# Moving the context norm behind the first latent products, pipelining the shifts in place, and spilling the values in 2 KB rows, in a hybrid attention layer

## The chip, the cores and the metric

The kernel runs on one core of one Trainium2 chip. The metric is the device time of one execution in microseconds (us). An execution is one launch of the whole layer: the inputs lie in the chip's memory, and the output is written back to it.

## The reference

One backbone layer over 512 latent tokens and 256 context tokens, all of width 2048, in f32. Two mixers read the same modulated norm: differential attention (8 heads of 128, two softmax maps per head) and multi-head latent attention (8 heads, low-rank q and kv). Behind them stand one output projection and a gated MLP with a depthwise convolution. Cut to what the change touches (the names are the reference's):

```python
mod_x = (silu(c) @ w_ada + b_ada)          # 6 x 2048: shift, scale, gate, twice
mod_c = (silu(c_ctx) @ w_ada + b_ada)      # the same for the context
h  = rmsnorm(x,   norm1_w) * (1 + s1)  + sh1     # latents,  512 x 2048
hc = rmsnorm(ctx, norm1_w) * (1 + s1c) + sh1c    # context,  256 x 2048
p  = h @ w_in ; pc = hc @ w_in                   # 3776 columns, one combined projection
q_da, k_da, v_da, c_q, c_kv, k_rope = split(p)   # the context's likewise
k_all = concat(context keys, latent keys) ; v_all = concat(context values, latent values)
w = softmax(q1 @ k1.T * a) - lam * softmax(q2 @ k2.T * a)     # per head
o_da = w @ v_all
x = x + g1 * (concat(rmsnorm(o_da) * .., o_mla) @ w_o)
h2 = rmsnorm(x, norm2_w) * (1 + s2) + sh2
x = x + g2 * ((silu(conv3(h2 @ w_up[:, :5632])) * (h2 @ w_up[:, 5632:])) @ w_down)
return rmsnorm(x, final_w)
```

## The kernel before

**Arithmetic.** Activations lie transposed, features on the 128 partitions, in 16 K-tiles (`kt`) of 128 features. A product of f32 accuracy is made of three: each operand is split into a high part (an ACT copy that rounds, lines 80, 210, 236, 386) and a low part (a DVE subtraction, lines 81, 213, 242, 389), and `mm3` issues high·high, high·low and low·high (lines 107, 108, 109). So nearly every weight block costs one 512 KB load by SP, one ACT cast, one DVE subtraction, and some tens of products on PE.

**Order.** The first stages stand inside `tc.manual_schedule`, which keeps on each engine the order in which the program issues the instructions. An engine works its list strictly in order, so what is written first runs first, and a late instruction holds up all behind it. Later stages, the attention and the output projection among them, are ordered by the scheduler of the language.

**Start.** SP loads the latents (16 tiles `xs`, 256 KB each), then the first rows of the scale weights (`scale_load`, 8 x 256 KB, tiles `adak`), two weight blocks and the 8 context tiles `cs`. ACT squares each tile (`sum_square`, lines 334 and 340), DVE adds the squares up in one tile (342), PE multiplies what is left with ones to sum over partitions (349), and `root` makes the reciprocal root `rinv`. The modulation's scale for a pair of K-tiles `u` is worked out by `scale_products(u)` on PE (285), a copy to `row` on ACT (290), `scale_turn` on PE (296) and `scale_out` on DVE (302).

**Projection of the first five column blocks (g0).** `g0_mm(kt, which)` (line 391) multiplies K-tile `kt` of the weights with the latents (`which` has 0) or the context (1), into PSUM tiles `lat0`, `ctx0`. It goes round by round, `u` = 0 to 7, two K-tiles a round. In each, DVE scales the next pair (`scaled`, 381), splits it (242; 244 where a shift is added) and makes the low parts of the weights (389).

**Row sums.** The shift of the modulation is a matrix-vector product on DVE: `row_sums` (line 260) multiplies a 1 MB row block of `w_ada` with the wide silu vectors `cb` (latents) and `ccb` (context) and sums along the row, 2.35 us each, 32 in all, one per K-tile and vector. The row blocks (tiles `ada`, two buffers, in POOL's queue) can't be loaded before the Silu of `ccb` is done, since a POOL copy into `gate` stands ahead of them in the queue. The K-tiles 8 to 15 get their shift with their split; 0 to 7 get it later, in place, by `add_shift` (line 594), before their products of the value columns. For the five g0 blocks, and the first half of block 5, which were multiplied without it, `bias_products` (line 643) multiplies the shift with those weights once more and adds it as a bias.

**Steps.** From there the projection goes in steps. `step(block, *tasks)` issues the products of weight block i, the cast of block i+2, the first task, the low part of block i+2, the load of block i+4, and then the other tasks. Steps 0 and 1 are `half_feature` (8.4 us each), steps 2 to 9 the eight `value_block`s, 10 and 11 `block(1,0)` and `block(1,1)`, 12 `block(2,0)`, then `bias_products(0)`, step 13 `block(2,1)`, and so on. The values of the first four heads, in six PSUM areas `v0` (two `b` tiles and the four halves of two `s` tiles), are split and written to the scratch array `v_d` by `put_value` (line 602) beside steps 10 and 11. A `gemv` (line 169) is the same as a row sum for the other modulation rows: 1 MB loaded, 2.4 us of DVE (174). 38 of them stand in the projection, each a task of a step (`gemvs(1)`). A small DVE instruction at line 1064 makes the scale of the second norm out of each.

**Later.** Attention reads v_d head by head (`da_head`, loads at line 872). The output projection (from line 1030 on) has weight blocks `w_o` of 5.44 us of PE each, with a gemv (`next_gemv(wo, 1)`, line 1046) before most of them; SP loads both.

## Time and profile before

| what | us |
|---|---|
| median of 3 runs (2431.09 to 2436.43) | 2435.21 |
| profiled execution | 2432.03 |
| its span, first to last instruction | 2430.2 |
| PE busy | 2332.7 (96%) |
| DVE busy | 1779.8 (73%) |
| ACT busy | 1102.3 (45%) |
| POOL busy | 273.2 (11%) |

The span and what lies around it (1.8 us) make the profiled execution. PE is busy in 96% of the span, and the granted TensorE clock is 0.989 on average. Rows of a timeline give start, duration (us), engine, line, operation, output and inputs, the shape, and in brackets how long the engine had stood idle before and which engine's instruction released it.

### The profile page before, as it was taken

To read this page: it belongs to the slowest core of one execution; us is meant where nothing else is said; L and a number is where in the kernel's file an instruction comes from. 1 tells how busy PE (TensorE), PEld (TensorE's weight loads), DVE (VectorE), ACT (ScalarE), POOL (GpSimd) and SP (SyncE) were. 2 spreads that over 40 slices of the span, in tenths; PEclk is the share of its full clock that TensorE was granted. 3 is DMA by queue.
4 is the path that set the end of the run, shared out by engine and by line. 5 is a ranking of instruction groups with operands and counts; after the bars stand their busy time and mean duration, and the time that the engine had idled before them with its cause. 6 is when DMAs were issued, how large, how long until landed. Compare 5 with 4: busy or idle time off the path is not lost.

```text
span 2430.2 us, 32271 instructions
## 1 busy us (share of the span) xinstructions
PE 2332.7 (96%) x12408; PEld 1962.5 (81%) x12408; DVE 1779.8 (73%) x2305; ACT 1102.3 (45%) x1660; POOL 273.2 (11%) x324
## 2 busy tenths in 40 slices
PE   5989799999999999989999999999999999999997
PEld 3777588777677778888888888888888888888887
DVE  5997577698868777587676767676766667676667
ACT  5222132255555542254454444454545445454553
POOL 0000100121200002100101011111111111111113
PEclk9999899999999999999999999999999999999999
DMA  9865877854411159723546555555555555555572
GB/s 356 298 234 192 299 253 285 281 158 119 134 51 44 44 212 372 260 83 114 152 118 156 121 156 122 156 122 156 122 154 124 147 131 141 137 137 141 133 214 79
DMA packets 139338, 407.45 MB, mean 168 GB/s; under 512 B 14752, under 2 KB 31664, under 8 KB 128560
## 3 DMA queue, kind: packets, MB, share of 16 engines
q1 hardware_dynamic: 105120, 298.42, 37.1%
q0 software_dynamic: 32912, 105.93, 18.2%
q8 instruction: 97, 1.59, 0.3%
q10 hardware_dynamic: 1152, 1.05, 0.1%
q14 instruction: 57, 0.47, 0.1%
HBM read 335.86 MB, written 69.48 MB: 167 GB/s over the span
## 4 chain that ended last, share of the span: by engine, by line
PE 78%; DVE 8%; issue 7%; DMA 3%; ACT 3%; POOL 1%; SPq 0%; DVEq 0%; POOLq 0%; ACTq 0%
PE y L1314 12%; PE b L108 9%; PE b L107 9%; PE b L109 9%; PE z L1314 6%; PE y L1316 6%; PE z L1316 3%; PE s L830 3%; PE x L1314 2%; PE s L108 2%; PE s L109 2%; PE s L107 2%; PE f L107 1%; PE x L1316 1%; PE pt L842 1%
## 5 line engine op out<-in xcount | busy, mean ns | idle before, releaser
L1335 POOL DMA_DIRECT2D x_d<-xs x160 | 140.4, 1014 | 1163.0 <-ACT xs L1334 1144.1
L107 PE MATMUL b<-ah,wh 128*128 128x512 f32 (+1 forms) x672 | 259.1, 386 | 0.0
L108 PE MATMUL b<-al,wh 128*128 128x512 f32 (+1 forms) x672 | 259.0, 385 | 0.0
L109 PE MATMUL b<-ah,wl 128*128 128x512 f32 (+1 forms) x672 | 258.0, 384 | 0.0
L1290 DVE TENSOR_TENSOR wl<-wr,wh 128x1024 fp32r<-128x1024 f32 x126 | 153.7, 1220 | 129.0 <-ACT wh L1284 129.0
L1290 DVE TENSOR_TENSOR wl<-rb,wh 128x1024 fp32r<-128x1024 f32 x124 | 151.1, 1219 | 127.9 <-ACT wh L1284 127.9
L1284 ACT CAST wh<-wr 128x1024 fp32r<-128x1024 f32 x126 | 132.3, 1050 | 206.1 <-PE b L108 100.4
L1284 ACT CAST wh<-rb 128x1024 fp32r<-128x1024 f32 x124 | 130.2, 1051 | 187.9 <-PE b L108 112.3
L1290 DVE TENSOR_TENSOR wl<-ws,wh 128x1024 fp32r<-128x1024 f32 x123 | 150.0, 1220 | 88.9 <-ACT wh L1284 88.9
L174 DVE CUSTOM_DVE_ANT_0 ada<-ada,cb,smt 128x2048 f32<-128x2048 f32 x64 | 153.7, 2405 | 55.0 <-DMA ada<-in_ada 54.1
L1284 ACT CAST wh<-ws 128x1024 fp32r<-128x1024 f32 x123 | 128.2, 1042 | 136.0 <-PE b L108 45.3
L109 PEld LDWEIGHTS b<-ah,wl 128*128 128x128 f32 x672 | 126.3, 188 | 25.6
L107 PEld LDWEIGHTS b<-ah,wh 128*128 128x128 f32 x672 | 126.6, 188 | 23.0
L108 PEld LDWEIGHTS b<-al,wh 128*128 128x128 f32 x672 | 126.6, 188 | 21.9
L107 PE MATMUL b<-a2k,wh 128*128 128x512 f32 (+1 forms) x352 | 136.5, 390 | 7.1 <-ACT a2k L1097 5.1
L109 PE MATMUL b<-a2k,wl 128*128 128x512 f32 (+1 forms) x352 | 134.3, 382 | 7.2 <-DVE wl L213 7.2
L80 ACT CAST wh<-wr 128x1024 fp32r<-128x1024 f32 (+2 forms) x64 | 64.3, 1005 | 135.0 <-PE b L108 42.9
L832 DVE TENSOR_REDUCE m<-s 128x1 f32<-128x768 f32 x96 | 90.2, 949 | 22.9 <-PE s L830 22.6
L1314 PE MATMUL y<-b2k,wh 128*128 128x512 f32 x410 | 106.9, 390 | 0.0
L210 ACT CAST wh<-wr 128x1024 fp32r<-128x1024 f32 x38 | 39.9, 1049 | 141.5 <-PE s L108 46.1
L1334 ACT ACTIVATE xs<-b,modx 128x512 f32<-128x512 f32 x160 | 101.1, 681 | 2.3 <-DMA x_d<-xs 1.9
L81 DVE TENSOR_TENSOR wl<-wr,wh 128x1024 fp32r<-128x1024 f32 (+2 forms) x64 | 78.3, 1223 | 32.3 <-ACT wh L80 31.9
(534 smaller groups left out, 6082.7 us busy)
## 6 DMA issues: line engine op xcount, KB each, us to landing
rb<-in_w_up SPq DMA_DIRECT2D x123, 512.0 KB, 4.5
ada<-in_ada POOLq DMA_DIRECT2D x54, 1024.0 KB, 5.6
wr<-in_w_dn SPq DMA_DIRECT2D x84, 512.0 KB, 4.0
x_d<-xs POOLq DMA_DIRECT2D x160, 256.0 KB, 6.0
wr<-in_w_up SPq DMA_DIRECT2D x53, 512.0 KB, 4.3
ada<-in_ada SPq DMA_DIRECT2D x26, 1024.0 KB, 6.7
wr<-in_w_f SPq DMA_DIRECT2D x34, 512.0 KB, 5.7
adak<-in_ada_k SPq DMA_DIRECT2D x64, 256.0 KB, 5.3
```

The source lines that it names most:

```text
L81: ve.tensor_tensor(dst_l, src, dst_h.bitcast(F32), op=ALU.subtract)
L107: pe.matmul(out, st[0], mv[0], start=start, stop=False, **kw)
L108: pe.matmul(out, st[0], mv[1], start=False, stop=False, **kw)
L109: pe.matmul(out, st[1], mv[0], start=False, stop=stop, **kw)
L174: ve.tensor_tensor_reduce(out=junk, in0=w, in1=vec, op0=ALU.mult, op1=ALU.add, scale=1.0, scalar=col("b_ada", j), accum_out=dst[:, j:j + 1])
L832: ve.tensor_reduce(out=m, in_=s[:, :TT], axis=AX.X, op=ALU.max, negate=True)
L1284: sc.copy(hi, raw)
L1290: ve.tensor_tensor(lo, raw, hi.bitcast(F32), op=ALU.subtract)
L1314: pe.matmul(o, w[j][0], hs[j], start=start and j == 0, stop=False, skip_group_check=True)
L1316: pe.matmul(o[:, h0], w[j][1], hs[j][:, h0], start=False, stop=j == 7, skip_group_check=True)
L1334: sc.mul(x, po, modx[:, 80 + dt:81 + dt])
L1335: gp.dma_start(x1_d[dt], x, accum_op=ALU.add)
```

## The change

Seven things are moved or reshaped; the arithmetic stays.

1. **Norm of the latents.** The last four squares go to PE directly, one ones-product each (345), so that DVE adds 11 tiles and not 14. The second half of the context loads comes behind `scale_load(1)`. `scale_products(0)` stands ahead of `root(0)`. `keep_warm` issues products of no use (cpad times ones, 7 x 512 columns, then 2 x 256 and 8 x 256) into a PSUM tile that is overwritten later.
2. **Norm of the context.** It moves behind the latent products of K-tiles 0, 1 and 2, and round 0 is folded into what comes before the loop. DVE adds all eight squares; `ctx_sum` needs two ones-products, where there were four. The Silu of `cb` and `ccb` comes behind the casts of K-tiles 2 and 3.
3. **Row sums.** Rounds 5 and 6 take two in place of three. In round 7 the low parts of the first two step blocks come ahead of their sums. More sums stand in step 0 and in the first value blocks.
4. **Shifts.** `add_shift` adds into a tile `sh` of its own, and issues the sums of the next pair before the low parts of the one before it; its K-tiles are spread over value blocks 1 to 5 as [0], [1], [2, 3, 4], [5, 6], [7], with row sums or gemvs in between.
5. **Values.** `v_d` is laid out as [high or low, key tile, 128, 512], so that one write has rows of 512 numbers, 2 KB, where a write had pieces of 128. A head's read becomes two reads with pieces of 128. Two of the six splits use tiles of their own (`rt`), in place of a pair that an earlier write must leave first.
6. **Bias weights.** Their loads are issued a step ahead (`bias_load`).
7. **Gemvs.** 36 stand in the projection, where 38 did; two move to the output projection, whose condition becomes `if kb != 7 if g else kb`.

```diff
@@ -338,28 +341,38 @@ the norms
-            if j < (15, 7)[i]:
-                ve.tensor_tensor(s, s, sq, op=ALU.add)
+            if i == 0 and j > 11:
+                pe.matmul(g0b[1], ones32, sq, start=j == 12, stop=False)
+                if j == KT - 1:
+                    pe.matmul(g0b[1], ones32, s, start=False, stop=True)
                 return
...
+            ve.tensor_tensor(s, s, sq, op=ALU.add)
+        def keep_warm(count, cols):
+            for _ in range(count):
+                pe.matmul(lat0[0][:, :cols], ones32, cpad.rearrange("p k i -> p (k i)")[:, :cols], start=True, stop=True)
...
+        keep_warm(7, 512)
         for kt in range(KT):
             sum_square(0, kt, xs[kt])
         sc.preload_act_table_set(tables)
+        scale_products(0)
+        scale_load(1)
+        ctx_load(range(4, 8))
+        keep_warm(2, 256)
         root(0)
-        scale_products(0)
         row = scale_row(0)
         scale_turn(0, row)
         scale_out(0)
+        keep_warm(8, 256)
@@ -406,27 +419,60 @@ ahead of the rounds
+        g0_mm(0, (0,))
+        scale_products(1)
...
+        g0_mm(1, (0,), (4, 0))
+        scale_turn(1, row)
+        g0_mm(1, (0,), (1, 2, 3))
...
+        ctx_sum()
         root(1)
+        g0_mm(2, (0,))
+        scale_products(2)
...
         g0_mm(0, (1,))
         g0_mm(1, (1,))
...
+        for wide in (cb, ccb):
+            sc.activation(wide, wide, AF.Silu)
+        sc.preload_act_table_set(tables)
         gp.tensor_copy(gate, ccb[:, 0:1])
         for kt in row_order[:2]:
             row_load(kt)
@@ -444,40 +490,32 @@ the rounds
-            elif u < NU - 1:
-                row_sums(3)
+            if u < NU - 1:
+                row_sums(3 if u < 5 else 2)
             else:
                 for i in range(2):
                     load(i)
                 for i in range(2):
                     cast(i)
-                    row_sums(2)
                     low(i)
                     load(i + 2)
-                row_sums(1)
+                    row_sums(2)
@@ -591,19 +629,27 @@ shifts and values
+    def add_shift(kts, between=None):
+        late = []
         for kt in kts:
...
+            t = kvs.tile([P, TT], F32, tag="kh", name=nm("sh"))
+            for hl, m, c in ((hx[kt], modx, slice(0, T)), (hc[kt], modc, slice(T, TT))):
+                ve.tensor_tensor(t[:, c], hl[0].bitcast(F32), hl[1].bitcast(F32), op=ALU.add)
+                high(hl, t[:, c], m[:, kt:kt + 1])
+                late.append((hl, t[:, c], m[:, kt:kt + 1]))
+            if len(late) > 2:
+                for _ in range(2):
+                    rest(*late.pop(0))
...
-            nc.sync.dma_start(v_d[half][:, :, i, t].rearrange("h p d -> p h d"), g.bitcast(F32))
+            nc.sync.dma_start(v_d[half][i, t], g.bitcast(F32))
@@ -725,16 +776,19 @@ steps 10 to 17
-        a, b, c, d, e_, f_ = lay(first)
-        step(block(1, 0), a, b, gemvs(1), c)
-        step(block(1, 1), d, gemvs(1), e_, f_, gemvs(1))
-        step(block(2, 0), feature_keys(1, gemvs(1)))
+        step(block(1, 0), lay(0), lay(5), gemvs(1), lay(1, True))
+        step(block(1, 1), lay(2), lay(3), gemvs(1), lay(4, True))
+        bias_load(0)
+        step(block(2, 0), gemvs(1), feature_keys(1))
         bias_products(0)
@@ -869,7 +923,9 @@ a head's values
-        nc.sync.dma_start(v.bitcast(F32), v_d[h // 4][h % 4])
+        for i in range(2):
+            nc.sync.dma_start(v[:, i].bitcast(F32),
+                              v_d[h // 4][i][:, :, h % 4 * P:(h % 4 + 1) * P].rearrange("t p d -> p t d"))
@@ -1042,7 +1098,7 @@ the output projection
-            if kb != 7 if g else kb > 2:
+            if kb != 7 if g else kb:
                 next_gemv(wo, 1)
```

How this moves the instructions shows at three places. The first is DVE's list at the end of the g0 rounds. `junk` and `ada` rows at line 260 are the row sums, the row at 389 (402 in the change) is the last low part of a g0 block, and the row at 213 the low part of step 0's weights. Before:

```order
L389 TENSOR_TENSOR wl_1301<-wr_1217,wh_1300 128x640
L260 ISA junk_1304,modx<-ada_1209,cb,smt 128x2048
L260 ISA modx 128x1
L260 ISA ada_1209,modc<-ada_1209,ccb,smt 128x2048
L260 ISA modc 128x1
L260 ISA junk_1309,modx<-ada_1294,cb,smt 128x2048
L260 ISA modx 128x1
L260 ISA ada_1294,modc<-ada_1294,ccb,smt 128x2048
L260 ISA modc 128x1
L260 ISA junk_1375,modx<-ada_1307,cb,smt 128x2048
L260 ISA modx 128x1
L213 TENSOR_TENSOR wl_1370<-wr_1365,wh_1369 128x1024
```

and in the change:

```order
L402 TENSOR_TENSOR wl_1317<-wr_1231,wh_1316 128x640
L260 ISA junk_1320,modx<-ada_1225,cb,smt 128x2048
L260 ISA modx 128x1
L260 ISA ada_1225,modc<-ada_1225,ccb,smt 128x2048
L260 ISA modc 128x1
L213 TENSOR_TENSOR wl_1384<-wr_1379,wh_1383 128x1024
```

Five sums stood between the two subtractions, and two stand there now; over all rounds 21 sums come before step 0's low part, and now 18.

The second place is DVE's list beside steps 10 to 12, where the values are split: rows at line 81 are the low parts of the values, from the PSUM tiles `s` and `b`, rows at 174 are gemvs, the one at 213 is a step's low part. Before:

```order
L81 TENSOR_TENSOR kl_2051<-s_1544,kh_2050 128x512
L1064 SCALAR_TENSOR_TENSOR a_93<-modx,smt 128x1 x2
L81 TENSOR_TENSOR kl_2108<-s_1544,kh_2107 128x512
L213 TENSOR_TENSOR wl_2105<-wr_1974,wh_2104 128x1024
L174 ISA ada_2116,modx<-ada_2116,cb,smt 128x2048
L174 ISA modx 128x1
L81 TENSOR_TENSOR kl_2120<-s_1545,kh_2119 128x512
```

and in the change:

```order
L81 TENSOR_TENSOR rt_2053<-s_1558,rt_2052 128x512
L1120 SCALAR_TENSOR_TENSOR a_93<-modx,smt 128x1
L81 TENSOR_TENSOR kl_2110<-s_1558,kh_2109 128x512
L213 TENSOR_TENSOR wl_2107<-wr_1976,wh_2106 128x1024
L81 TENSOR_TENSOR kl_2119<-s_1559,kh_2118 128x512
L174 ISA ada_2124,modx<-ada_2124,cb,smt 128x2048
L174 ISA modx 128x1
```

The third split goes to tiles `rt` of its own and no longer needs the `kl` of the first; the split of the second `s` tile's first half now stands ahead of a gemv.

The third place is SP's list at the change to the second half of the output projection: `ada` rows are 1 MB gemv rows, `wr` rows the weight blocks. Before:

```order
L171 DMA ada_7890<-in_ada 128x2048
L171 DMA ada_7957<-in_ada 128x2048
L89 DMA wr_7960<-in_w_o 128x1024
L171 DMA ada_7990<-in_ada 128x2048
L89 DMA wr_7993<-in_w_o 128x1024
L1055 DMA xr_7945<-in_x_t 128x512
```

and in the change:

```order
L171 DMA ada_7840<-in_ada 128x2048
L171 DMA ada_7873<-in_ada 128x2048
L89 DMA wr_7976<-in_w_o 128x1024
L171 DMA ada_7906<-in_ada 128x2048
L171 DMA ada_7973<-in_ada 128x2048
L1111 DMA xr_7961<-in_x_t 128x512
L89 DMA wr_8009<-in_w_o 128x1024
L171 DMA ada_8006<-in_ada 128x2048
L171 DMA ada_8039<-in_ada 128x2048
L89 DMA wr_8042<-in_w_o 128x1024
```

Two rows of 1 MB stand between neighbouring weight blocks at two places, where one stood.

More of the change, by code (lines that the diff above doesn't have):

```diff
@@ L147, in layer_kernel @@
     k_d = [dram.tile([2, P, TT], F32, name=f"k_d{h}") for h in range(NH)]
-    v_d = [dram.tile([4, P, 2, NKEY, P], F32, name=f"v_d{i}") for i in range(2)]
+    v_d = [dram.tile([2, NKEY, P, 512], F32, name=f"v_d{i}") for i in range(2)]
     def apply_rope(out, ps, tmp):
@@ L306, in layer_kernel, with ctx_load @@
         raws_ = [wraw(w_g0[kt], 640) for kt in range(2)]
-        for i in range(8):
-            cs.append(c2k())
-            nc.sync.dma_start(cs[i], ctx_t[i])
-        scale_load(1)
+        def ctx_load(n_):
+            for i in n_:
+                cs.append(c2k())
+                nc.sync.dma_start(cs[i], ctx_t[i])
+        ctx_load(range(4))
         sc.activation(cpad[:, :, 0:2], smt[:, OFF["cc"]:OFF["cc"] + 2 * KT].rearrange("p (k i) -> p k i", i=2), AF.Silu)
@@ L420, in layer_kernel @@
             rest(*parts(kt, 1))
-        scale_products(1)
-        row = scale_row(1)
         g0_mm(0, (1,))
-        scale_turn(1, row)
-        scale_out(1)
         g0_mm(1, (1,))
+        row = scale_row(2)
+        scale_turn(2, row)
+        g0_high(raws_[1])
+        scaled(3, 0)
+        high(*parts(3, 0))
+        g0_low(3, raws_[1])
+        rest(*parts(3, 0))
+        scale_out(2)
+        for kt in (2, 3):
+            scaled(kt, 1)
+        for kt in (2, 3):
+            high(*parts(kt, 1))
+            rest(*parts(kt, 1))
+        for wide in (cb, ccb):
+            sc.activation(wide, wide, AF.Silu)
+        sc.preload_act_table_set(tables)
         gp.tensor_copy(gate, ccb[:, 0:1])
@@ L429, in layer_kernel @@
             row_load(kt)
+        gp.dma_start(silu_c, cb[0:1])
         def next_tokens(u):
@@ L641, in step, with bias_load @@
         steps.append(i)
+    bw = {}
+    def bias_load(n_):
+        bw[n_] = sp_.tile([P, D], F32, tag="ada", name=nm("bw"), bufs=2)
+        if n_ == 3:
+            gp.dma_start(bw[n_][:, :1024], w_f[0, 0])
+        else:
+            for i, kt in enumerate(range(3 * n_, min(3 * n_ + 3, KA))):
+                gp.dma_start(bw[n_][:, i * 640:(i + 1) * 640], w_g0[kt])
     def bias_products(n_):
```

112 lines of the change are left out of this document (55 added, 57 removed).

## The prediction

> **What bounds the kernel now.** I read the page's busy shares first, then the waits of PE in the first 450 us, where all of the change but two pieces lies, then PE's timeline at each wait.
>
> ```profile
> PE 2332.7 (96%) x12408; PEld 1962.5 (81%) x12408; DVE 1779.8 (73%) x2305; ACT 1102.3 (45%) x1660; POOL 273.2 (11%) x324
> ```
>
> PE is busy in all but 97.5 us of the span, and only products taken from PE, gaps of PE or a low clock can give time back. The change takes away no product of the layer, so it is worth what it closes of gaps.
>
> ```profile
> PE b L349 <- DVE tmp L342: 18.2, 1, 18.2
> PE s L107 <- DVE kl L81: 7.8, 1, 7.8
> PE b L109 <- DVE wl L213: 7.2, 1, 7.2
> PE b L660 <- DVE a L1064: 6.7, 1, 6.7
> PE b L108 <- DVE wl L213: 2.5, 1, 2.5
> ```
>
> Each row is who waits, for whom, the sum, the count and the longest. All five are in pieces that the change edits, and each is a single wait at a known place:
>
> ```profile
> 18.17 2.08 PE L349 MATMUL b<-tmp,ones 128*128 128x512 f32 x2 [18.17 <-DVE tmp L342]
> 28.14 0.79 PE L107 MATMUL b<-a2k,wh 128*128 128x512 f32 x1 [1.98 <-ACT a2k L236]
> 33.06 0.63 PE L107 MATMUL s<-a2k,wh 128*128 128x512 f32 x1
> 33.49 0.63 PE L108 MATMUL s<-a2k,wh 128*128 128x512 f32 x1
> 35.18 0.40 PE L107 MATMUL b<-a2k,wh 128*128 128x512 f32 x1
> 35.42 0.39 PE L108 MATMUL b<-a2k,wh 128*128 128x512 f32 x1
> 138.68 0.40 PE L108 MATMUL b<-a2k,wh 128*128 128x512 f32 x1
> 146.25 0.80 PE L109 MATMUL b<-a2k,wl 128*128 128x512 f32 x1 [7.18 <-DVE wl L213]
> 150.69 0.40 PE L107 MATMUL b<-a2k,wh 128*128 128x512 f32 x1
> 200.24 0.50 PE L108 MATMUL b<-wl,a2k 128*128 128x512 f32 x1 [2.54 <-DVE wl L213]
> 258.32 0.55 PE L107 MATMUL s<-c2k,wh 128*128 128x256 f32 x1 [7.81 <-DVE kl L81]
> 275.26 1.94 PE L660 MATMUL b<-bw,bias 128*32 128x512 f32 x6 [6.73 <-DVE a L1064]
> ```
>
> Products stand 0.43 us apart at 33.06 (clock low) and 0.24 at 35.18 (clock full): a long wait costs some 0.2 us for each product after it. From 146.25 to the first full-speed row at 150.69 these are 4.4 us, about ten products, 2.0 us.
>
> **A: the start to step 0, 146.25 us.** Which engine paces this stretch?
>
> ```profile
> 60.00:130.00 70.00, 68.36 (x488) 55.42 (x487) 67.84 (x94) 21.16 (x41) 3.72 (x7) 1.00 0.80 279
> 130.00:147.00 17.00, 9.82 (x53) 8.22 (x53) 16.19 (x17) 6.85 (x13) 1.59 (x3) 0.91 0.70 243
> 72.27 0.46 DVE L302 TENSOR_SCALAR a<-b,b,smt 128x2 f32<-128x2 f32 x2
> 132.69 2.34 DVE L260 CUSTOM_DVE_ANT_0 junk<-ada,cb,smt 128x2048 bf16<-128x2048 f32 x1
> 144.98 1.22 DVE L213 TENSOR_TENSOR wl<-wr,wh 128x1024 fp32r<-128x1024 f32 x1
> ```
>
> In the window rows the third and fifth numbers are PE and DVE. Both are nearly full to 130; then PE runs out and DVE has 16.19 of 17 us. The five sums from 132.69 on stand ahead of the low part at 144.98 for which PE waits 7.18 us. So DVE ends this stretch, and two things move its end. First, three sums fewer stand ahead of that low part (18, were 21): 3 x 2.4 us (2.35 and the read of the accumulator) = 7.2. Second, DVE's sums can start earlier, because they wait for the row that is loaded after the silus:
>
> ```profile
> 7.87 10.24 DVE L342 TENSOR_TENSOR tmp<-tmp,sq 128x512 f32<-128x512 f32 x13 [0.72 <-ACT sq L340]
> 55.01 1.28 ACT L467 ACT_TABLE_LOAD   x1
> 58.13 1.89 ACT L467 ACTIVATE ccb<-ccb 128x2048 f32<-128x2048 f32 x1
> 65.34 2.34 DVE L260 CUSTOM_DVE_ANT_0 junk<-ada,cb,smt 128x2048 bf16<-128x2048 f32 x1
> ```
>
> Here ccb is ready at 60.0 and the first sum starts 5.3 us later, a row's landing. In the change: 11 additions of 0.79 us in place of 14 end at about 16.6, the last square and a product of 0.95 us put PE's sum near 19.1 (21.95 now), the scales no longer stand behind it, and the first block's third product starts near 26.3 (30.1 now), warm if the keep-warm products keep the clock, which saves 15 x 0.2 = 3.0. Then three latent passes of 3.45, two scale products of 1.9 and eight context groups end near 45.4; the scale row, turn and two scaled tiles take 2.8, the table and the silus 5.1: ccb at 53.3, 6.7 earlier, of which I count 6.2 at DVE's first round (72.7 to 66.5). In all 6.2 + 7.2 = 13.4, so the low part is done at 132.8. Can PE be there? Its last product before the wait ends at 139.1; an earlier start (25.9, was 28.14) and the 3.0 of warm clock make this 133.9, and it stood idle 3.9 us more between 28 and 60 and 1.6 between 60 and 130, which the context's move may close, down to 128.4. DVE's own gaps in the two window rows are 3.0 us. Bounds for the low part: 133.9, PE closing none, and 129.8, DVE closing all. I take 132.8. With the 2.0 us of slow products that go with the wait, **A = 15.4**.
>
> **B: the value blocks.** The 2.54 us at 200.24 is a low part queued behind shifts and sums on DVE. The change spreads them, and low parts no longer wait for ACT between each pair; but it also brings the three later sums into these steps, less two gemvs, +2.4 us of DVE, which was busy 68 of 86 us there. I keep a new wait of 1 us: **B = 1.5** (bounds -1 to 2.5).
>
> **C: values, steps 10 to 13.**
>
> ```profile
> 252.26 0.69 DVE L81 TENSOR_TENSOR kl<-s,kh 128x512 fp32r<-128x512 f32 x1 [5.06 <-DMA v_d<-kl]
> 257.48 0.69 DVE L81 TENSOR_TENSOR kl<-s,kh 128x512 fp32r<-128x512 f32 x1 [4.40 <-DMA v_d<-kl]
> v_d<-kl SPq DMA_DIRECT2D x8, 256.0 KB, 7.1
> k_d<-kh SPq DMA_DIRECT2D x8, 384.0 KB, 2.9
> ```
>
> PE's 7.81 us is a chain: the PSUM tile for block (2,0) is free when its last value is split, the splits wait for tiles that earlier writes of v_d leave, and those take 7.1 us for 256 KB, in 512-byte pieces. k_d's rows are 3 KB and took 2.9 us for half as much again. With 2 KB rows, and with two of six splits in own tiles, a write has a whole step of 8.4 us to land: the 5.06 and 4.40 go, and the 7.81 with them. The bias products' 6.73 has a different cause: the copies of the shift stand on DVE behind a gemv and a low part. The loads of their weights go ahead (0.46 us of waiting now), but that gemv and that low part are still there, 2.35 + 1.22 = 3.6 us: I keep a wait of 3.6 (bounds 0 and 6.73). Slow products after both waits, at 0.2 each, were about 3.2 us. 7.81 + 6.73 + 0.46 + 3.2 - 3.6: **C = 14.6** (bounds 11.5 to 18.2).
>
> The Trainium skill ("TensorE: Matmul & The Clock Gate", section "Part 1: The HAM clock gate (the "warmup" mystery)") says that about 3.4 us of idling lower the clock and about 3.4 us of work raise it. The trace has 4.4 us for the raising, and 2.54 us at 200.24 lowered nothing. By the rule the kept wait of 3.6 us could just cool PE, and C would be about 1.4 smaller.
>
> **D: the output projection.** Two gemvs more stand there, ahead of its weights in SP's queue.
>
> ```profile
> 910.00:1010.00 100.00, 100.00 (x443) 82.81 (x442) 79.85 (x66) 25.36 (x28) 26.15 (x19) 1.00 0.95 361
> 901.37 1.06 ACT L80 CAST wh<-wr 128x1024 fp32r<-128x1024 f32 x1 [9.62 <-DMA wr<-in_w_o]
> ada<-in_ada POOLq DMA_DIRECT2D x54, 1024.0 KB, 5.6
> ```
>
> PE is full here and the DMA engines are at 0.95, with casts already waiting for weights (9.62 us at 901.37), so the cover is thin. 2 MB at 361 GB/s are 5.8 us of transfers; some 3 us of weights stand ready, and I take **D = -2.5**. Bounds: 0, if the two rows land in gaps, and -11.2, two whole landings. DVE had 20 us to spare in these 100, so the 4.8 us of sums are free.
>
> **The rest at nothing.** The keep-warm products lie in PE's first idle 18 us and while it waits for rinv and the scales; were they to run late they cost PE their own time, at most 8 x 0.2. The two ones-products fewer for the context are in A. The values' reads become two issues of 0.4 us in a queue where each head's load came far ahead of its use:
>
> ```profile
> 473.06 0.33 SPq L872 DMA_DIRECT2D v<-v_d  x1
> 497.56 0.39 PE L107 MATMUL po<-wth,v 128*128 128x512 f32 x1
> v<-v_d SPq DMA_DIRECT2D x8, 768.0 KB, 5.0
> DMA to landing us min/median/max: 2.2/8.3/11.9
> ```
>
> 24.5 us of cover for a landing of 5.0. No row shows a read in 512-byte pieces; the nearest are the writes of v_d in such pieces, 256 KB in 2.2 to 11.9 us beside steps 10 to 12 (the last row), a third of a head's bytes. Three times 2.2 is 6.6; three times 11.9 is 35.7, which is not hidden (R3). Most of the 8.3 is time in a queue with others, so I take the short end.
>
> **Sum.** 15.4 + 1.5 + 14.6 - 2.5 = 29.0. Against the profiled 2432.03 that is 2403.0. The median of the runs is 3.2 above the profiled execution, so the median should be **2406**.
>
> **Rivals.**
>
> *R1: the front does not move, since DMA paces it.* Latents, weights, context, scale rows and the wide vectors, some 22 MB, have to arrive before the first row sum, and the rows of scale weights keep SP full.
>
> ```profile
> 10.00:20.00 10.00, 1.83 (x2) 0.84 (x3) 7.08 (x11) 7.34 (x11) 0.00 (x0) 1.00 1.05 406
> 28.00:60.00 32.00, 28.12 (x158) 20.30 (x159) 18.80 (x38) 16.28 (x26) 2.00 (x4) 0.84 0.91 353
> ```
>
> The last two numbers are the DMA engines' share and the GB/s. At 406 the first row can land near 59, in time for the 66.5 above; at 353 it lands near 67. Then DVE's 6.2 us is lost and only its queue order counts: gain 22.8, time **2412**. Against it: 353 is a mean with slack in it. The Trainium skill ("DMA: Bandwidth & Descriptors", section "Where 436 GB/s comes from") puts the memory's limit for one core at about 358 GB/s, which speaks for R1; the 406 of the window above is over it, so here the trace disagrees.
>
> *R2: the output projection pays in full.* D = -11.2 and not -2.5: **2415**. For it: DMA at 0.95, casts already late. Against it: PE had no gap there.
>
> *R3, slower: the values' reads in 512-byte pieces come too late.* If one takes T us from issue to landing, PE stands 8 x (T - 24.5) us. The gain of 29.0 is used up at T = 28.1; T = 30 makes **2450**, and T = 35.7 makes 2496. Against it: T would have to be over five times today's 5.0, for all eight heads.
>
> *R4: the keep-warm products don't do what their name says*, or delay the sum behind them: PE starts the first block where it does now, and A loses start and clock (6.2 + 3.0): **2415**.
>
> *More: neither of the new waits of 1.0 and 3.6 comes*, and D is 0: gain 36, time 2399; at the edge of the likeliest case.
>
> **How the numbers follow.** The forecast 62%, with its own range 2398 to 2415; R1 16%, R2 10%, R4 5%; R3 3%; 4% for what I don't see, a wait made by the new order of loads or sums. A difference under 0.2%, 4.9 us, can't be told from none with these measurements. All cases but R3 and half of the last are faster by far more: faster 0.94, same 0.02, slower 0.04. The range 2395 to 2420 takes in A to C at their better ends and R1, R2 and R4.
>
> **What would show it.** A: PE's wait for the low part at step 0 falls below 1 us, and step 0's third product starts between 130 and 134; ccb is ready near 53; the products from 26 on stand 0.23 us apart. If ccb stays near 60, R1 or R4. B: no wait over 1 us before 230. C: no DVE subtraction waits for a write of v_d, no wait of PE for a split, and 0 to 3.6 us at the bias products. D: PE's gaps at 890 to 920 show ACT waiting for `w_o` behind `ada`. R3: products of `po` that wait for `v`. I am wrong outright if the gain is under 12 or over 40 us, or if a wait on a row of `ada` in the first rounds takes the place of the one removed.

## The result and the profile after

The changed kernel takes 2421.1 us (median of 8 runs, 2418.0 to 2429.1), the kernel before 2435.3 (8 runs): a ratio of 0.9949, interval 0.9935 to 0.9962. By the medians that is 14.2 us faster (12.4 by the ratio), where 29 were forecast; the time lies 1.1 us over the range's end. Measured once more on another occasion the ratio is 0.9932 (0.9916 to 0.9948).

The profiled execution of the changed kernel, 2425.63 us, lies 4.5 above its median, and that of the kernel before 3.2 under its own, so the two profiles are only 6.4 us apart. A second profile of the changed kernel (2421.85 us) stands beside the first in the table. It gives the time at which PE reaches the same piece of work. The first row is the second less the wait that ends there.

| PE reaches | before | after | after, again | gain | gain, again |
|---|---|---|---|---|---|
| end of block (2,0), step 12 | 268.5 | 242.9 | 244.5 | 25.7 | 24.0 |
| first bias product | 275.3 | 251.9 | 252.7 | 23.4 | 22.5 |
| sums of the ckv squares | 352.8 | 331.7 | 331.9 | 21.1 | 20.9 |
| first attention scores | 466.0 | 448.6 | 447.2 | 17.4 | 18.8 |
| last transposes of the attention | 863.1 | 848.4 | 848.8 | 14.7 | 14.3 |
| first y product of the MLP | 1123.8 | 1118.1 | 1114.3 | 5.7 | 9.5 |
| end of the span | 2430.2 | 2423.9 | 2420.1 | 6.3 | 10.1 |

At step 12 PE is nearly as early as the forecast wanted it. Then the lead is handed back in steps. The waits of PE over the whole changed kernel, the view that was read of the kernel before, name the places (`issue`: no release that the profile shows):

```profile
PE b L716 <- issue: 9.0, 1, 9.0
PE b L285 <- DVE a L302: 6.2, 1, 6.2
PE s L357 <- ACT cpad L314: 5.5, 1, 5.5
...
PE s L614 <- ACT nq L606: 4.6, 1, 4.6
...
PE b L107 <- ACT wh L80: 3.9, 2, 2.5
```

Four of the five old waits are gone: 18.2 at the sum of the squares, 7.8 at the split of the values, 7.2 and 2.5 at the low parts. Of the first, only 5.5 us stand as a wait (357), because keep-warm products, which are of no use to the layer, fill the rest; the gain there is that the sum of the squares is done at 18.5 us and not at 21.9. The bias products (now line 716) wait 9.0 us in place of 6.7, and there are three new waits: for the scales in the first rounds (285), for the ckv squares (614) and for weights of the output projection (line 80).

The last rows of the table come from the groups of the tiles y and pt, before and after (duration in ns, then first and last start):

```profile
L842 PE MATMUL pt<-ident,w x176: 270/272/273, 698.5 to 863.1; 128*128 128x128 f32 x176
L1314 PE MATMUL y<-a2k,wh x328: 389/389/398, 1123.8 to 2350.3; 128*128 128x512 f32 x164
```

```profile
L896 PE MATMUL pt<-ident,w x176: 270/272/274, 683.9 to 848.4; 128*128 128x128 f32 x176
L1370 PE MATMUL y<-a2k,wh x328: 389/389/398, 1118.1 to 2344.0; 128*128 128x512 f32 x164
```

From the last transposes to the first y product, which is in the main the output projection, the kernel before needs 260.7 us and the changed one 269.7.

### The profile page after: what moved, and what is told of

It is laid out like the page before. It is cut to its first block, busy times and chain, and to the rows that moved or that the text cites. A ratio compares the mean times of both kernels' runs of the same rounds, so it can differ in the third digit from the quotient of the medians.

```text
span 2423.9 us, 32339 instructions
## 1 busy us (share of the span) xinstructions
PE 2342.3 (97%) x12444; PEld 1968.2 (81%) x12444; DVE 1775.2 (73%) x2303; ACT 1100.8 (45%) x1660; POOL 271.7 (11%) x322
## 4 chain that ended last, share of the span: by engine, by line
PE 81%; DVE 8%; issue 5%; ACT 3%; DMA 2%; POOL 1%; SPq 0%; DVEq 0%; ACTq 0%; POOLq 0%
PE y L1370 13%; PE b L107 10%; PE b L108 9%; PE b L109 9%; PE z L1370 6%; PE y L1372 6%; PE z L1372 3%; PE s L884 3%; PE s L108 3%; PE s L107 3%; PE s L109 3%; PE x L1370 2%; PE x L1372 1%; PE f L107 1%; PE pt L896 1%
## 5 line engine op out<-in xcount | busy, mean ns | idle before, releaser
L108 PEld LDWEIGHTS b<-al,wh 128*128 128x128 f32 x672 | 126.6, 188 | 21.9
L886 DVE TENSOR_REDUCE m<-s 128x1 f32<-128x768 f32 x96 | 90.3, 949 | 26.5 <-PE s L884 26.1
L210 ACT CAST wh<-wr 128x1024 fp32r<-128x1024 f32 x38 | 40.0, 1052 | 128.8 <-PE b L109 53.8
```

What stands on the lines that cost most here:

```text
L108: pe.matmul(out, st[0], mv[1], start=False, stop=False, **kw)
L886: ve.tensor_reduce(out=m, in_=s[:, :TT], axis=AX.X, op=ALU.max, negate=True)
```

## The experiments

The theory after the comparison: the change does to PE's waits what was forecast, but three things take from it: the bias products, whose shift is copied behind a late gemv; the 1 MB rows of gemvs, which pass through two buffers and give DVE a pace of its own; and the output projection with two more rows. The main rival: PE's lead would be capped by the same pace whatever is done to the order. Every kernel was timed against the kernel before, in three groups; ratios are to that kernel.

**The changed kernel again**, unaltered.

> The changed kernel once more, unaltered, as the yardstick of this group. Its eight runs spread from 2418.0 to 2429.1, the kernel before's only from 2431.1 to 2436.4. If the spread is made in the output projection (waits for weights behind two more gemv rows), this profile has another sum of waits there than the 3.9 us of the first, and all else within 1 us. If it is made at the start (landing of the first row), the first row sum moves away from 62.1. Time 2418 to 2427, 11 to 16 under the kernel before.

Measured: 2421.0 us, ratio 0.9932 (0.9916 to 0.9948). The profile moves from the first one by up to 1.7 us at steps 0 to 12 (the first row sum starts at 63.5 and not at 62.1), and by 4.2 us in the output projection (265.5 for 269.7). Both places that the expectation names move. So a difference of 2 us at one place of one profile says little, and comparisons below rest on ratios and on larger shifts.

**The copies of the shift ahead of step 12.**

```diff
+        bias_copies()          # memset and the two copies, taken out of bias_products(0)
         step(block(2, 0), gemvs(1), feature_keys(1))
```

> The two copies of the shift that the bias products read are issued before step 12, ahead of the gemv whose row lands late; nothing else. Theory: the 9.0 us wait at the bias products hangs on these copies alone, so it falls under 1 us, PE no longer cools there (another 1.4), the row behind the freed weights buffer is loaded some 9 us earlier, and the wait of 4.6 at the ckv squares shrinks: 7 to 11 us faster than the changed kernel. Rival: DVE paces steps 13 to 20 through late gemv rows whatever PE does; then the 9.0 comes back as a wait at the ckv squares and the gain is under 3 us.

Measured: 2423.1, ratio 0.9947 (0.9934 to 0.9961), not faster than the changed kernel. PE's waits from 230 to 345 us:

```profile
PE b L719 <- DVE a L1123: 5.5, 1, 5.5
PE s L614 <- ACT nq L606: 4.6, 1, 4.6
```

The first bias product starts at 243.6, 8.3 us earlier, but the group ends at 273.0, as before (273.6), and the squares come at 331.1 (331.7). The rival holds: the wait moved, and the pace did not. The 5.5 us end at 250.1, when DVE has read block 1's PSUM tile for the keys (lines 152 and 153, until 250.0); that work stands behind the same late gemv, so the likely reason is that the second tile of the bias products isn't free before. What sets the pace shows in the changed kernel on POOL, whose queue issues the loads (the bracket says which release the issue waited for), and on DVE, which uses them:

```profile
227.34 1.60 POOL L697 DMA_DIRECT2D bw<-in_w_g  x3 [4.27 <-DVE modx L174]
235.84 0.53 POOL L171 DMA_DIRECT2D ada<-in_ada  x1 [6.90 <-DVE modx L174]
246.71 1.59 POOL L697 DMA_DIRECT2D bw<-in_w_g  x3 [10.01 <-DVE modx L174]
254.57 0.53 POOL L171 DMA_DIRECT2D ada<-in_ada  x1 [6.27 <-PE b L717]
```

```profile
244.05 2.35 DVE L174 CUSTOM_DVE_ANT_0 ada<-ada,cb,smt 128x2048 f32<-128x2048 f32 x1 [6.74 <-DMA ada<-in_ada]
247.47 0.68 DVE L152 TENSOR_TENSOR rt<-b,ropet 128x512 f32<-128x512 f32 x1
251.62 0.17 DVE L705 COPY bias<-modc 128x8 f32<-128x8 f32 x1
259.72 2.35 DVE L174 CUSTOM_DVE_ANT_0 ada<-ada,cb,smt 128x2048 f32<-128x2048 f32 x1 [7.93 <-issue]
```

Bias weights and gemv rows are the same tag with two buffers. The weights taken at 227.34 keep one buffer until PE's products after 251.89; every gemv row must go through the other: issued at 235.84 when the last gemv leaves it, landed 8 us later, summed at 244.05. That buffer then goes to the next weights (246.71), so the next row is issued only when PE frees the first ones (254.57). The rows at 247.47 and 251.62 are the start of the keys' work (lines 152 to 562) and the second copy of the shift: the copies stand behind the gemv, the low part and some 4 us of keys' work. DVE's sum at 259.72, the first of step 13, stands 20.2 us before the sum at that place of the kernel before (279.88). From 300 to 332 us DVE is busy for 29.61 of 32 us, and ACT's squares wait for its keys' work, so the squares are 21 us earlier and not 26.

**The loads of the bias weights beside their products again.**

```diff
-        bias_load(0)             # and 1, 2, 3: a step ahead
         step(block(2, 0), gemvs(1), feature_keys(1))
 ...
+        bias_load(n_)            # in bias_products
         spad, w = raws["b"][0], bw[n_]
```

> The changed kernel with the loads of the bias weights back beside their products, in place of a step ahead. Theory: a load a step ahead holds one of the two 1 MB buffers for a whole step, so the gemv row behind it starts late (DVE waits 6.7 us for it at 237 to 244) and the bias copies with it; late loads give that buffer to the row: the row's wait falls under 3 us, the bias products' wait from 8.2 and 9.0 to 4 to 7. Rival: POOL's queue is in order, so the weights then come late themselves and PE waits for them as long: no gain, or up to 4 us lost.

Measured: 2416.2, ratio 0.9922 (0.9910 to 0.9934). PE's waits from 230 to 345 us are one row:

```profile
PE b L717 <- issue: 3.1, 1, 3.1
```

The squares come at 323.2 with no wait, 8.5 us before the changed kernel's. DVE's waits for rows from 215 to 300 us, first in the changed kernel, then here:

```profile
DVE ada L174 <- DMA ada<-in_ada: 20.9, 6, 6.7
DVE ada L174 <- issue: 9.6, 2, 7.9
```

```profile
DVE ada L174 <- DMA ada<-in_ada: 16.3, 8, 4.8
```

30.5 us of waiting became 16.3 (15.7 in the kernel before, same stretch). By the trace, loading the bias weights a step ahead, part 6 of the change, was a loss. In time it is 0.10 or 0.27% by the point values, 2.4 to 6.6 us; the interval is just clear of the first measurement of the changed kernel and overlaps with the second.

**Six gemvs left out of steps 12 to 15.**

```diff
-        step(block(2, 0), gemvs(1), feature_keys(1))
+        step(block(2, 0), lambda: None, feature_keys(1))
 ...                          # likewise (2,1): two, (3,0): one, (3,1): two
```

> The changed kernel without the six gemvs of steps 12 to 15 (the last six K-tiles of the last gate are set to zero). Theory: DVE's idle time from 237 to 296 us is made by rows of 1 MB that pass through two buffers, which the bias weights share; without the six, the bias products' wait of 9.0 falls to under 1, DVE reaches step 16 before PE, and the wait of 4.6 at the ckv squares goes: the ckv squares come at 318 to 322 in place of 331.7, and attention starts 9 to 13 us earlier; of that 4 to 10 us are left at the end. Rival: the order on DVE alone makes it, rows or not: squares not before 328.

Measured: 2408.9, ratio 0.9891 (0.9876 to 0.9906). The squares come at 325.7 (expected 318 to 322) without a wait, attention starts at 439.2, 8.0 and 9.4 us earlier than in the two profiles of the changed kernel. The profile is that of its slowest run (2417.09), so these places may lie late. The bias products still wait 5.9 us: with no gemv in the way the copies stand behind the keys' work, which itself starts late:

```profile
245.37 0.69 DVE L153 TENSOR_TENSOR rt<-b,ropet 128x512 f32<-128x512 f32 x1 [5.56 <-issue]
```

The profile names no release here. The tile `rt` has two buffers, and the change's own tiles for two of the splits (part 5) come from them: the writes of v_d out of them are issued at 235.1 and 238.6 and land 10.2 and 7.1 us later, so the likely cause is that `rt` is not free before. So the rows are one cause, and the copies' place on DVE behind the keys is a second. In ratios the six rows are worth 0.4 to 0.6%, 10 to 14 us, some 2 us a row.

**All of it at once**: copies early, the first two rows early (below), the six gemvs and the output projection's two left out.

> The changed kernel with the copies of the shift early, the first two rows issued early, and eight gemvs left out (six of steps 12 to 15, two of the output projection; the last eight K-tiles of the last gate are set to zero). Theory: with rows and their order out of the way, what the change does to PE's waits is worth the 29 us that were forecast: 27 to 36 us under the kernel before, ckv squares at 312 to 317, attention from 430 to 436. Rival: the early places each cost as much as they save (early copies alone gained nothing): not more than the 26 us of the run without six rows.

Measured: 2399.1, ratio 0.9850 (0.9837 to 0.9862), 36.7 us under the kernel before. PE has no listed wait between 230 and 345 us, DVE none for a row from 215 to 300; the squares come at 315.8, the attention at 429.1. That is the forecast's gain and more, but of a kernel with eight rows fewer. By this, what was missing in the changed kernel is in the rows and their order; what the eight rows cost by themselves is in the 36.7 too, and no run separates it.

**The first two rows issued early.**

```diff
+        gp.tensor_copy(gate, ccb[:, 0:1])
+        for kt in row_order[:2]:
+            row_load(kt)
         for wide in (cb, ccb):
             sc.activation(wide, wide, AF.Silu)
```

> POOL's gate copy reads ccb before its silu in place of after it, so that the first two rows of 1 MB are issued some 8 us earlier. Theory: DVE's 3.6 us wait for the first row (62.1) goes, the first sum starts near 58.6, the wait of PE for the scales at 69.6 falls from 6.2 to under 3, and step 0's third product comes 3 us earlier: 2 to 4 us faster than the changed kernel. Rival (DMA supply paces the front): the two rows only delay the scale weights and g0 weights by the same bytes; no gain, or a loss of up to 3 us.

Measured: 2420.0, ratio 0.9932 (0.9919 to 0.9945): the same as the changed kernel again (0.9932). The mechanism is there, and the order is that of the kernel before, where the copy into `gate` stood ahead of the Silu. In the changed kernel ccb is ready at 53.1, the rows are issued at 53.8, and the first sum starts 8.3 us later:

```profile
51.24 1.90 ACT L470 ACTIVATE ccb<-ccb 128x2048 f32<-128x2048 f32 x1
53.82 1.33 POOL L251 DMA_DIRECT2D ada<-in_ada  x2 [0.43 <-issue]
62.12 2.35 DVE L260 CUSTOM_DVE_ANT_0 junk<-ada,cb,smt 128x2048 bf16<-128x2048 f32 x1 [3.59 <-DMA ada<-in_ada]
69.59 3.64 PE L285 MATMUL b<-adak,cpad 128*32 128x256 f32 x32 [6.20 <-DVE a L302]
```

Issued at 45.1 the rows are there in time; the first sum starts at 61.06, since DVE now waits for weights (58.64 after 2.45 us), whose cast on ACT waited 2.44 us for their load, not for a row; and PE's wait of 6.2 us falls to at most 1.0. PE is 3 us earlier at the bias products (249.0) and 6 to 7 at the first scores (441.5). But from the last transposes to the first y it needs 270.8 us, the longest of all, and the lead is gone at the end.

**Without the keep-warm products** (all three calls removed).

> The changed kernel without its 17 groups of keep-warm products. Theory: PE then runs the sum of squares and the first block slow; products stand 0.43 us apart at 26 in place of 0.22, and the first block's end, the context norm and the silus come 2 to 4 us later; since the first rows land some 8 us after the silus and pace DVE from there, all of it goes through to step 0: 2 to 4 us slower than the changed kernel. Rival: DMA supply paces the front, and nothing is seen at step 0: within 1 us.

Measured: 2421.1, ratio 0.9946 (0.9932 to 0.9960): no difference from the changed kernel. At the front it is as expected: the first block's third product at 28.3 and not 26.1, its first three products of 0.80, 0.79 and 0.63 us for 0.58, 0.39 and 0.39, the first row sum at 66.1 for 62.1. At the bias products 2.6 us of that are left, at the squares 0.8, at the end nothing. The expectation that it goes through to the end fell.

**Sums ahead of the low parts again, in round 7.**

```diff
                     cast(i)
+                    row_sums(2)
                     low(i)
                     load(i + 2)
-                    row_sums(2)
```

> The changed kernel with the low parts of the first two step blocks behind their two row sums again, as before the change. Theory: two sums of 2.4 us stand ahead of the low part again, so PE waits for it some 4.7 us at step 0 and cools, and that is what this reordering saves: 4 to 7 us slower than the changed kernel at step 0; if the rows of 1 MB pace what comes later, less than half of that is left at the end. Rival: all of it is left, 4 to 7 us.

Measured: 2426.4, ratio 0.9973 (0.9962 to 0.9984). PE waits 4.1 us for the low part at step 0 and is 5 to 6 us late at the bias products. In ratios it is 0.24 to 0.41% slower than the changed kernel, 6 to 10 us: by this nothing of it was swallowed, against the theory and with the rival. The profile, taken from its fastest run, doesn't show the way there: at the last transposes (850.0) only 1.2 to 1.6 us of the delay are left. So this two-line move is the one piece of the change that, by the ratios, reaches the end in full; the places of one profile don't confirm it.

**The old layout of v_d** in the changed kernel.

```diff
-            nc.sync.dma_start(v_d[half][i, t], g.bitcast(F32))
+            nc.sync.dma_start(v_d[half][:, :, i, t].rearrange("h p d -> p h d"), g.bitcast(F32))
```

> The changed kernel with the old layout of v_d: writes in 512-byte pieces, one read of 768 KB a head. Theory: the own tiles for two of the six splits already cover slow writes, and the writes' landing (6.8 to 7.8 in the changed kernel, 5.6 and 7.1 before) did not get shorter, so the layout alone is worth nothing: within 2 us of the changed kernel. Rival: the layout removed the 7.8 us wait; then a wait of PE for a split of 3 to 8 us returns at step 12.

Measured: 2423.5 of a group whose kernel before has 2434.1, ratio 0.9959 (0.9945 to 0.9972). By the point values 2.4 to 6.6 us slower than the changed kernel, though the intervals overlap. In its profile, which is of its slowest run (2428.88), a wait of 2.3 us for a split returns at step 12 and the bias products come 6 us later. So neither expectation: the layout is worth something, though not the whole 7.8 us. Its mechanism is not the landing; see the last section.

**The output projection's two gemvs.** Once put back into steps 23 and 25 of the input projection, once left out:

```diff
-            if kb != 7 if g else kb:
+            if kb != 7 if g else kb > 2:
```

> The two gemvs of the output projection's first half go back into the input projection (steps 23 and 25, where PE had no gaps). Theory: the two 1 MB rows are what makes ACT wait for weights there, so PE's waits of 1.5 and 2.5 us at 899 and 908 and the slow clock after them go: 4 to 6 us faster than the changed kernel, and a smaller spread of the times. Rival: the output projection's start moved 14.7 us towards the attention's end and its weights are late for another reason: waits stay, under 1.5 us of gain.

> The changed kernel without the two gemvs that moved to the output projection: they are left out altogether (the last two K-tiles of the last gate are set to zero), so nothing takes their place. Theory: the output projection is paced by its 16 MB of weights and its rows of 1 MB, and two rows fewer give back what the stage lost (265.5 and 269.7 us from the attention's last transposes to the first y product, 260.7 in the kernel before): 4 to 9 us faster than the changed kernel. Rival: the stage is long because it starts earlier and its weights' first loads don't: under 2 us.

Measured: put back 2425.1, ratio 0.9955 (0.9941 to 0.9968); left out 2415.6, ratio 0.9922 (0.9909 to 0.9934). The stage from the last transposes to the first y is 262.8 us with the two put back and 263.2 with them left out. In ten profiles with 28 rows in it (the changed kernel twice and eight of its variants) it is 265.5 to 270.8, mean 268.6. So two rows cost the stage 5.4 us, as two times 1 MB at the 361 GB/s of the forecast's window (5.8 us) would. In the changed kernel ACT waits for weights at the change to the second half:

```profile
898.31 1.04 ACT L80 CAST wh<-wr 128x1024 fp32r<-128x1024 f32 x1 [3.21 <-DMA wr<-in_w_o]
906.65 1.04 ACT L80 CAST wh<-wr 128x1024 fp32r<-128x1024 f32 x1 [6.76 <-DMA wr<-in_w_o]
```

But put back, they cost the projection more: attention starts at 453.5, 5 to 6 us later than in the changed kernel, with 3.4 us of waiting for k_d. The expected gain of 4 to 6 us did not come: the ratio is 0.06 to 0.23% higher, within the intervals. Some 2.5 us of the stage remain (263.2 with 26 rows, 260.7 in the kernel before): with the two left out, PE's wait for the MLP's first weights is 2.7 us for 1.4, and PE is busy 253.8 us for 252.4, at a granted clock of 0.97 for 0.98.

**A candidate** that computes the whole layer: copies early, first rows early, bias loads late.

> All of the layer computed: the changed kernel with the copies of the shift early, the first two rows issued early, and the loads of the bias weights beside their products. If the buffers pace the bias stage, PE's waits there sum to under 4 us and attention starts 5 to 9 us earlier than in the changed kernel; the output projection gives some of it back: 2 to 6 us faster than the changed kernel. If the rows pace it whatever the order, within 2 us of it.

Measured: 2413.8, ratio 0.9912 (0.9899 to 0.9925): 22.0 us faster than the kernel before by the medians. That is 0.37% less than the first ratio of the changed kernel (0.9949), whose interval is clear of it, and 0.20% less than the second (0.9932), whose interval overlaps between 0.9916 and 0.9925. PE's waits from 230 to 345 us sum to 3.6:

```profile
PE b L719 <- DMA bw<-in_w_g: 3.3, 2, 3.1
PE b L720 <- DVE a L1120: 0.3, 1, 0.3
```

The attention starts at 438.5, 9 to 10 us earlier than in the changed kernel; the stage behind it takes 266.9.

## Why the prediction was right in direction and wrong in size

**A, 15.4: too large by a fifth to a third.** Step 0's low part and third product in the changed kernel:

```profile
134.27 1.22 DVE L213 TENSOR_TENSOR wl<-wr,wh 128x1024 fp32r<-128x1024 f32 x1
136.04 0.39 PE L109 MATMUL b<-a2k,wl 128*128 128x512 f32 x1
```

The third product is 10.2 us earlier (8.6 in the second profile), with the 2.0 of slow products 10.6 to 12.2. The first block's third product (26.1, forecast 26.3) and ccb (53.1, forecast 53.3) came as worked out. The step that failed is "ready at 60.0 and the first sum starts 5.3 us later, a row's landing". It was no landing. In the kernel before, POOL copies into `gate` ahead of the Silu, and issues the first two rows long before it:

```profile
41.18 0.77 POOL L251 DMA_DIRECT2D ada<-in_ada  x1 [1.79 <-PE b L285]
43.16 0.55 POOL L251 DMA_DIRECT2D ada<-in_ada  x1 [1.21 <-DVE rinv L167]
```

They land 7.1 and 8.3 us later, and the sum at 65.34 waits for none; DVE comes to it from the splits of K-tiles 2 and 3. So what was said of the row sums ahead of the prediction, that the row blocks can't be loaded before the Silu of `ccb`, holds for the changed kernel only. There part 2 puts the Silu ahead of that copy, the rows are issued at 53.82, 12.6 us later, and the first one lands 8.3 us after that, no slower than before. DVE is through with the splits at 58.5, 5.4 us after ccb and near what was worked out, and then waits 3.59 us for the row. The forecast took the order for the same in both kernels and charged the move with nothing; its own last sign of being wrong, a wait on a row of `ada` in the first rounds, came. The DMA engines have a part in it:

```profile
28.00:60.00 32.00, 28.45 (x220) 21.31 (x219) 18.92 (x38) 17.52 (x28) 2.00 (x4) 1.00 1.02 385
```

They stand at 1.02 of a share and 385 GB/s, where they had 0.91 and 353, and with the rows issued early DVE waits 2.45 us for weights instead. So R1 was half true: DVE's lead was 3.2 us and not 6.2 (4.3 with the rows early). And it had a consequence that I had not priced: the scales of a pair stand behind DVE's sums, so PE, early, waits 6.2 us for them at 69.6. The sum's other step, three row sums fewer ahead of the low part for 7.2 us, held, and its larger part was isolated by putting two of them back.

**B, 1.5: too small.** Past the wait at 69.6, none of PE over 0.6 us is left up to 242 us; the kept wait of 1 us did not come.

**C, 14.6: the values right, the bias products wrong.** The 7.8 us wait and its slow products went, though two of DVE's splits still wait 1.9 and 1.0 us for writes of v_d. The kept wait of 3.6 was 9.0 (8.2 in the second profile), outside the bounds of 0 and 6.73. The bounds were taken from what stood before, and the change's own part 6 was credited with 0.46 us and charged nothing. What it cost was a buffer: I had looked at what the weights' load waits for, not at who else uses its tag. With late loads the wait is 3.1 us, near the kept 3.6, but that is luck: there the gemv and the low part are done before PE comes, and what it waits for is the keys' work, DVE's from 242.15 to 246.5, which the 3.6 had left out.

**D, -2.5: -5.4, and 2.5 more in the stage.** The 5.8 us of transfer that I had worked out was the right price, and the 3 us of cover that I set against it wasn't there. R2, the stage paying in full, describes the mechanism; its -11.2 was too much.

**The sum itself.** It adds what each wait of PE gives back. Up to step 12 that worked out: A, B and the 7.8 of the split are 24.7 us, and the table has 25.7 and 24.0. (A's shortfall of 3 to 5 us doesn't show there, partly by luck: B's extra 1.0 and the slow products behind the 7.8, which the forecast counts with C's 3.2, are about as much.) The bias products should have begun 27.8 us early or more (6.7 less 3.6 on top), and began 23.4 and 22.5 early. So the larger part of what is missing is lost from the bias products on, not in the front. Behind step 12 the waits no longer add: the rows through two buffers give DVE a lead of 20.2 us, and what PE has over that, it waits off at the squares. The run with all reliefs (36.7) fits with the terms adding up when the rows do not pace, but it has eight rows fewer. Of the lead at the first scores, 2.7 and 4.5 us go in the attention, which the forecast took as unchanged; the two profiles show a lower clock there (last section), and why stays open.

**Rivals.** R3 did not come: no wait for v is in the changed kernel, and the reads in 512-byte pieces landed in 4.7 us (median), so the short end was right. R4 did not come either: the front's products are warm with the keep-warm products and slow without, though the end does not notice. The rival that would have held, one buffer ring shared by early loads and rows, I did not have.

## What to carry to other kernels

A load that is issued earlier costs a buffer for all the time that it lies there; with two buffers in a ring, look at who else must pass through the ring, before crediting the earlier load with anything. When a sum is made of waits of the busiest engine, ask at each later stage whether the next engine's supply (here 1 MB rows, 1 to 4 us of time each by the runs that left them out or moved them) moves forward by as much; the lead over it is lost at the next meeting point. And before a gap in front of an instruction is called a load's landing, look for the load's issue in its queue: here the row had been issued 24 us before the sum that seemed to wait for it, and the change that moved its issue was priced at nothing.

## What the hardware showed that was not expected

Writes of v_d in 2 KB rows did not land much sooner, by the median. From issue to landing, min, median and max in the stretch of the first heads' values, in the kernel before, in the changed kernel, and in the changed kernel with the old layout:

```profile
DMA to landing us min/median/max: 2.2/8.3/11.9
```

```profile
DMA to landing us min/median/max: 6.1/7.7/9.4
```

```profile
DMA to landing us min/median/max: 4.4/6.6/12.6
```

What differs is the time that SP's queue spends on issuing one (ns, min/median/max), in the changed kernel and with the old layout:

```profile
L652 SPq DMA_DIRECT2D v_d<-kh x4: 319/324/437, 220.0 to 232.5; - x4
L652 SPq DMA_DIRECT2D v_d<-rt x4: 320/320/530, 225.5 to 237.3; - x4
```

```profile
L652 SPq DMA_DIRECT2D v_d<-kh x4: 381/1188/2902, 221.8 to 241.2; - x4
L652 SPq DMA_DIRECT2D v_d<-rt x4: 360/619/4104, 231.6 to 244.7; - x4
```

0.3 us became 0.4 to 4.1, and the longest landing goes from 9.4 to 12.6. The fourfold number of pieces can't be the whole reason: in the kernel before, with the same pieces, the median is 0.36 to 0.38 us (the longest 2.4). I take it, without having tested it alone, that the queue's time is what the layout saves; what makes it long stays open.

The second is the clock. After a wait of PE the next products are slow or not, and the length of the wait alone does not decide it. After 2.54 us (before, 200.24) they ran at full speed, after 4.11 us (sums ahead of the low part, step 0) they did not. At the ckv squares two waits of one length went both ways, first with the sums ahead of the low part, then without keep-warm products; the eight products take 2.85 us in the one and 4.54 in the other:

```profile
336.86 2.85 PE L614 MATMUL s<-nq,ones 128*128 128x512 f32 x8 [2.86 <-ACT nq L606]
332.54 4.54 PE L611 MATMUL s<-nq,ones 128*128 128x512 f32 x8 [2.85 <-ACT nq L603]
```

After 2.31 us (old layout, step 12) the first five products ran at full speed, and those from 240.11 to 243.10 were slow:

```profile
239.20 0.35 PE L107 MATMUL s<-c2k,wh 128*128 128x256 f32 x1 [2.31 <-DVE kl L81]
241.18 0.63 PE L107 MATMUL b<-a2k,wh 128*128 128x512 f32 x1
```

So the keep of 3.6 us that the forecast made in C could have cooled PE, as the Trainium skill ("TensorE: Matmul & The Clock Gate", section "Part 1: The HAM clock gate (the "warmup" mystery)") has it with a window of about 3.4 us; here 2.31 us were followed by a low clock once, and 2.86 us once were not.

The third is the clock in the attention. From the first scores to the last transposes, the same products take 396.7 to 398.0 us in five of the fourteen profiles, the kernel before among them, and 399.2 to 401.6 in the other nine, both of the changed kernel among them. The first kind has a granted clock of 1.00, the second 0.98 or 0.99; before and after:

```profile
466.00:863.10 397.10, 376.41 (x1942) 294.55 (x1943) 321.19 (x510) 222.59 (x425) 40.53 (x34) 1.00 0.33 100
448.60:848.40 399.80, 379.27 (x1941) 296.71 (x1942) 321.38 (x510) 222.74 (x425) 40.56 (x34) 0.99 0.33 100
```

PE's idle time is the same, 20.7 and 20.5 us, and its busy time is 2.9 us longer. What makes the clock lower there, no run shows.
